# The opening of a two-layer trunk: first modulation on TensorE, early fillers, one-piece scaling

## The chip, the cores and the metric

The kernel runs on one core of one Trainium2 chip. The metric is the device time of one execution, in microseconds; the time of a kernel is the median of its runs.

A core has five engines, each with its own stream of instructions: PE multiplies matrices, DVE and ACT work on tiles element by element (ACT with a table of functions that has to be loaded), POOL is a third such engine, and SP here only issues transfers. Transfers from memory (DMAs) can be issued by SP, ACT and POOL; each issuer has its own queue. Engines meet only where one needs what another has written, or where a buffer has to be given back first.

## The reference

Two layers work on x, 256 tokens by 1024 channels. Each has a token mixer (layer 0 dilated attention, layer 1 gated linear attention) and a gated convolutional feed-forward part. Ahead of each of these four parts x is normalised and modulated by a vector c:

```python
for i in range(DEPTH):                                  # 2 layers
    mod = jax.nn.silu(c) @ w_ada[i] + b_ada[i]          # c: 1024 -> 6 * 1024
    sh1, sc1, g1, sh2, sc2, g2 = split(mod, 6)
    h = rmsnorm(x, norm_mix[i]) * (1.0 + sc1) + sh1
    y = dilated_mixture(h, ...) if i == 0 else gla_mixer(h, ...)   # first step: h @ w_in
    x = x + g1 * y
    h = rmsnorm(x, norm_ffn[i]) * (1.0 + sc2) + sh2
    x = x + g2 * conv_ffn(h, ...)
return rmsnorm(x, norm_final)
```

All data are fp32. What matters here is the start: the mean of squares of x, SiLU of c, the shift and the scale (pieces 0 and 1 of `mod`) of layer 0, and the first columns of h @ w_in, which are the queries, keys and values of the first pair of heads.

## The kernel before

**Layout.** Channels lie on the 128 partitions, tokens along the row. x is one tile `x_all` of 128 x 8 x 256: 8 tiles (kt = 0 to 7) of 128 channels. A weight block for one kt is 128 x 1920 and comes from memory into a buffer of the pool `wraw` (4 buffers, `raw`; the modulation weights `ada_raw` use the same four).

**Products.** A product in fp32 is made of three in the faster format fp32r: each operand is split into a high part and a remainder (`whi`/`wlo` of the weights, `hhi`/`hlo` of h), and high·high, high·low and low·high are summed in PSUM, the memory that PE writes. The weights' high part is a cast on ACT (`split`, L176), the remainder a subtraction on DVE (`low_part`, L188), each in two halves of 960 columns. `mm3` (L203 to L205) is the three products of one block.

**The opening.** c comes as one row of 1024 on one partition (ACT's queue, L86). PE multiplies it by a row of ones, so that all 128 partitions hold all of c (`cb`, L125); ACT applies SiLU (`c_bc`, L126). x comes in two transfers on SP's queue. DVE and ACT square it (L389, L392), DVE adds tiles up (L395), PE sums over partitions with a matrix of 1/1024 (`ms`, L215), and ACT makes `rstd` of it by a logarithm and an exponential (L217, L219); these two need another function table (`exp_ln_after`) than SiLU. Between these, PE makes products that nobody reads (`keep_warm`, L301): three blocks of 4, 3 and 6, and three small products for the rows of the attention's biases (L409), which ACT copies out (L437).

**A step of kt.** SP loads `ada_raw` and `raw`. DVE makes two dot products of 128 x 1024 with `c_bc` (`ada_dot`, L142), one for the scale, one for the shift; ACT makes one column of each (L150, L152). DVE scales x by the column and by `rstd` (`xr`, L287), ACT adds the shift and rounds to the high part `hhi` (L289), DVE makes the remainder `hlo` (L291). PE then makes this tile's products: 6 blocks of 256 columns for queries and keys, three products each (L696), 2 of 384 for the values (L700), and 6 of `mm3`.

**Order.** A scheduler puts the instructions of each engine in the order in which their inputs are due; `with behind(a):` holds an instruction back until `a` has been placed, without a wait on the chip. Transfers of one issuer run in the order written. Banks of PSUM belong to three tags (p: 2, s: 3, t: 3); where `bank` is called without a tag, the next of a fixed cycle is taken.

Of the kernel before, what the change touches and what calls it, by code (L numbers as in the profile page):

```python
# [59 lines left out]
def trunk(ctx: ExitStack, tc: tile.TileContext, I, out):  # L60
# [18 lines left out]

    def exp_ln_after(last):  # L80
# [15 lines left out]
    nc.scalar.dma_start(tab[:32, :], I["rel_bias"])  # L96
    nc.vector.memset(tab[32:33, :], 1.0)
    oh = wspl.tile([P, 2048], F32, tag="whi", name="oh")
    nc.scalar.dma_start(oh[:33, :NROW], I["onehot"])
# [6 lines left out]
    eps = const.tile([P, 1], F32, name="eps")  # L106
    nc.vector.memset(eps, EPS)
    ident = const.tile([P, P], F32, name="ident")
    make_identity(nc, ident)
# [11 lines left out]

    c_bc = const.tile([P, D], F32, name="c_bc")
    for n in range(2):
        ps = bank("cb", "t")
        last_c = mm(ps, ones_d[:1, :], c_row[:1, 512 * n : 512 * n + 512], start=True, stop=True)  # L125
        silu = nc.scalar.activation(c_bc[:, 512 * n : 512 * n + 512], ps, AF.Silu, scale=float(D))  # L126
# [11 lines left out]
    def ada_dot(l, n, s, raw):  # L138
# [5 lines left out]
        )  # L144
        m = state.tile([P, 1], F32, tag=f"mod{l}{piece}{kt}", name="mod")
# [8 lines left out]
        return i, j  # L154
# [119 lines left out]
    @contextmanager  # L274
    def behind(*those):

        with ExitStack() as st:
            for i in those:
                st.enter_context(tc.issue_after(i.ins))
            yield  # L280

# [15 lines left out]
    def keep_warm(n):  # L297

        ps = bank("warm")
        for i in range(n):  # L300
            mm(ps[:, :P], ones_d, ones_d, start=True, stop=True)  # L301

    early_x = [state.tile([P, T + 16], F32, tag=f"ex{k}", name="early_x") for k in range(KT)]
# [78 lines left out]

    sq = wspl.tile([P, 2048], F32, tag="wlo", name="sq").rearrange("p (k t) -> p k t", k=KT)
    with behind(last_c):
        keep_warm(4)
    nc.vector.tensor_tensor(sq[:, 0:4, :], x_all[:, 0:4, :], x_all[:, 0:4, :], op=ALU.mult)  # L389
    with behind(silu):  # L390
        for i in (4, 6):
            last_sq = nc.scalar.activation(sq[:, i : i + 2, :], x_all[:, i : i + 2, :], AF.Square)  # L392
    for n in (0, 4):
        for m in (2, 1):
            last_add = nc.vector.tensor_tensor(sq[:, n : n + m, :], sq[:, n : n + m, :], sq[:, n + m : n + 2 * m, :], op=ALU.add)  # L395
        if n == 0:
            with behind(last_add):
                last_add = scale_terms(0)
    exp_ln_after(last_sq)
    r = rstd_of([sq[:, 0, :], sq[:, 4, :]])  # L400

    rows_ps, at = [], 0
    with behind(norm_ops[0]):
        keep_warm(3)
        for i, (g, n) in enumerate(ROWS):
            c = slice(at, at + n)
            ps = bank("rows", "t")[:16, 0:n]
            rows_ps.append((ps, c))
            last_row = mm(ps, tab[:, 16 * g : 16 * g + 16], oh[:33, c], start=True, stop=True)  # L409
            at += n  # L410
    with behind(last_row):
        keep_warm(6)


    w0, h = [], []
    last = last_add
    for kt in range(KT):
        ada = ada_load(0, kt, 1 if kt else 2)
        with behind(*((last,) if kt else (norm_ops[1], last))):
            dots = [ada_dot(0, kt, 0, ada)]  # L420
        with behind(dots[0][0]):
            dots.append(ada_dot(0, kt, 1, ada))

        def between(scaled, high):

            ahead, term = (dots[1][1], dots[1][1]) if kt == 0 else (dots[0][1], dots[1][1])
            w0.append(split(I["w0"][kt], 15 * P, 1 if kt else 2, after=((ahead,), (high,)), lows=False))
            with behind(scaled):
                return [low_part(w0[-1], 0)]

        h.append(normed(0, 0, r, kt, (dots[1][0],), between))
        with behind(chain[kt][1]):
            last = low_part(w0[kt], 1)
        if kt == 0:
            with behind(copied[0]):
                for ps, c in rows_ps:
                    nc.scalar.copy(rows[:, c], ps)  # L437
        if kt == 1:
            with behind(last):
                last = scale_terms(1)  # L440
    with tc.issue_after(last_load[0].ins):
        nc.sync.dma_start(rows_d, rows)
        nc.sync.dma_start(small[:, C_CW:], I["small"][:, C_CW:])
# [226 lines left out]
    for u in range(NPAIR):  # L670
# [13 lines left out]
        if u == 0:  # L684
            b0 = [bank("pqk", tg) for tg in "ssspp"]
            pqk = [b[:, T * i : T * i + T] for b in b0[:3] for i in range(2)]
            pv = b0[3:]
            b1 = [bank("pqk", "t") for _ in range(3)]
            pqk1 = [b[:, T * i : T * i + T] for b in b1 for i in range(2)]
            for kt in range(KT):  # L690
                s, e = kt == 0, kt == KT - 1

# [803 lines left out]
```

## Time and profile before

| what | value |
|---|---|
| time, median of 3 runs | 747.81 us (747.49 to 748.27) |
| profiled execution | 752.01 us |
| its span, first to last instruction | 750.2 us |
| PE busy | 741.7 us, 99% |
| DVE busy | 648.2 us, 86% |
| ACT busy | 480.6 us, 64% |
| POOL busy | 31.7 us, 4% |
| DMA | 187.20 MB, mean 250 GB/s |
| granted TensorE clock, mean | 0.998 |

The span is of one execution under the profiler, 4.2 us longer than the median of the runs. Busy means that an instruction is under way; a PE that runs at a low clock, or makes products that nobody reads, is as busy as one that works. A row of an engine's order of time gives start, length (both us), engine, line and operation, output <- inputs, sizes, and the number of records put together. In brackets stands how long the engine had waited and for what. "PEld" rows are loads of the stationary operand. The granted clock is a column of the profile that stands apart from the durations.

### The profile page before, as it was taken

To read this page: it belongs to the slowest core of one execution; us is meant where nothing else is said; L and a number is where in the kernel's file an instruction comes from. 1 tells how busy PE (TensorE), PEld (TensorE's weight loads), DVE (VectorE), ACT (ScalarE), POOL (GpSimd) and SP (SyncE) were. 2 spreads that over 40 slices of the span, in tenths; PEclk is the share of its full clock that TensorE was granted. 3 is DMA by queue.
4 is the path that set the end of the run, shared out by engine and by line. 5 is a ranking of instruction groups with operands and counts; after the bars stand their busy time and mean duration, and the time that the engine had idled before them with its cause. 6 is when DMAs were issued, how large, how long until landed. Compare 5 with 4: busy or idle time off the path is not lost.

```text
span 750.2 us, 15928 instructions
## 1 busy us (share of the span) xinstructions
PE 741.7 (99%) x6344; PEld 726.6 (97%) x6344; DVE 648.2 (86%) x1195; ACT 480.6 (64%) x943; POOL 31.7 (4%) x57
## 2 busy tenths in 40 slices
PE   8999999999999999999999999999999999999997
PEld 5999999999999999999999999999999999999996
DVE  6997998989988859999998886898969999997592
ACT  5556775555656658776766565865768766666551
POOL 0002001101101010000000000000010000000100
PEclk9999999999999999999999999999999999999999
DMA  9998789888788438877746997776757766874621
GB/s 349 399 304 294 241 317 369 270 315 280 263 309 284 132 117 295 311 281 240 256 128 207 315 341 243 256 266 224 261 194 274 281 223 236 211 179 157 205 100 57
DMA packets 39481, 187.20 MB, mean 250 GB/s; under 512 B 9020, under 2 KB 11708, under 8 KB 25838
## 3 DMA queue, kind: packets, MB, share of 16 engines
q1 hardware_dynamic: 39024, 185.73, 71.4%
q8 instruction: 50, 0.82, 0.4%
q10 hardware_dynamic: 382, 0.45, 0.2%
q14 instruction: 25, 0.20, 0.1%
HBM read 185.06 MB, written 1.10 MB: 248 GB/s over the span
## 4 chain that ended last, share of the span: by engine, by line
PE 98%; DVE 1%; ACT 0%; DMA 0%; issue 0%; DVEq 0%; ACTq 0%
PE pab L204 10%; PE pab L205 10%; PE pab L203 10%; PE pqk L203 6%; PE pqk L205 6%; PE pqk L204 6%; PE pd L204 5%; PE pd L205 5%; PE pd L203 5%; PE pv L203 4%; PE pv L205 4%; PE pv L204 4%; PE pqk L696 2%; PE py L203 2%; PE py L205 2%; PE py L204 2%
## 5 line engine op out<-in xcount | busy, mean ns | idle before, releaser
L176 ACT CAST whi<-raw 128x1024 fp32r<-128x1024 f32 (+4 forms) x264 | 237.8, 945 | 107.0 <-PE pab L204 55.0
L182 DVE TENSOR_TENSOR wlo<-raw,whi 128x1024 fp32r<-128x1024 f32 (+5 forms) x248 | 263.8, 1092 | 30.6 <-ACT whi L176 29.8
L205 PE MATMUL pab<-hhi,wlo 128*128 128x256 f32 x672 | 185.0, 276 | 0.0
L204 PE MATMUL pab<-hlo,whi 128*128 128x256 f32 x672 | 184.9, 277 | 0.0
L203 PE MATMUL pab<-hhi,whi 128*128 128x256 f32 x672 | 183.1, 277 | 0.0
L204 PEld LDWEIGHTS pab<-hlo,whi 128*128 128x128 f32 x672 | 126.1, 188 | 0.2
L205 PEld LDWEIGHTS pab<-hhi,wlo 128*128 128x128 f32 x672 | 126.2, 188 | 0.0
L203 PEld LDWEIGHTS pab<-hhi,whi 128*128 128x128 f32 x672 | 125.1, 188 | 0.1
L142 DVE CUSTOM_DVE_ANT_0 ada_raw<-ada_raw,c_bc 128x1024 f32<-128x1024 f32 x96 | 114.3, 1230 | 4.6 <-DMA ada_raw<-in_w_ada 4.4
L203 PE MATMUL pqk<-hhi,whi 128*128 128x256 f32 x374 | 102.4, 279 | 0.0
L204 PE MATMUL pqk<-hlo,whi 128*128 128x256 f32 x374 | 101.8, 277 | 0.0
L205 PE MATMUL pqk<-hhi,wlo 128*128 128x256 f32 x374 | 101.3, 278 | 0.0
L205 PE MATMUL pd<-ghi,wlo 128*128 128x256 f32 x308 | 84.9, 276 | 0.0
L204 PE MATMUL pd<-glo,whi 128*128 128x256 f32 x308 | 84.9, 276 | 0.0
L203 PE MATMUL pd<-ghi,whi 128*128 128x256 f32 x308 | 84.7, 276 | 0.0
L203 PEld LDWEIGHTS pqk<-hhi,whi 128*128 128x128 f32 x374 | 69.9, 188 | 0.2
L204 PEld LDWEIGHTS pqk<-hlo,whi 128*128 128x128 f32 x374 | 69.9, 188 | 0.0
L205 PEld LDWEIGHTS pqk<-hhi,wlo 128*128 128x128 f32 x374 | 69.2, 188 | 0.1
L204 PEld LDWEIGHTS pd<-glo,whi 128*128 128x128 f32 x308 | 57.8, 188 | 0.0
L205 PEld LDWEIGHTS pd<-ghi,wlo 128*128 128x128 f32 x308 | 57.8, 188 | 0.0
L203 PEld LDWEIGHTS pd<-ghi,whi 128*128 128x128 f32 x308 | 57.7, 188 | 0.0
L204 PE MATMUL pv<-wlo,hhi 128*128 128x384 f32 (+2 forms) x160 | 52.8, 332 | 0.0
(272 smaller groups left out, 1440.8 us busy)
## 6 DMA issues: line engine op xcount, KB each, us to landing
raw<-in_w_up SPq DMA_DIRECT2D x42, 1024.0 KB, 4.9
ada_raw<-in_w_ada SPq DMA_DIRECT2D x29, 1024.0 KB, 6.0
raw<-in_w_down SPq DMA_DIRECT2D x28, 704.0 KB, 5.1
ada_raw<-in_w_ada SPq DMA_DIRECT2D x38, 512.0 KB, 6.8
raw<-in_wqk SPq DMA_DIRECT2D x18, 1024.0 KB, 6.7
raw<-in_wv SPq DMA_DIRECT2D x14, 768.0 KB, 7.0
raw<-in_w SPq DMA_DIRECT2D x7, 960.0 KB, 6.1
raw<-in_w_v_b SPq DMA_DIRECT2D x6, 768.0 KB, 5.0
```

Of the source, the lines that this page charges most:

```text
L142: i = dotted[0] = nc.vector.tensor_tensor_reduce(w, w, c_bc, op0=ALU.mult, op1=ALU.add, scale=1.0, scalar=0.0, accum_out=dot,)
L176: copied[0] = nc.scalar.copy(part(hi[:, c]), part(raw[:, c]))
L182: last_lo[0] = nc.vector.tensor_tensor(part(lo[:, c]), part(raw[:, c]), part(hi[:, c].bitcast(F32)), op=ALU.subtract)
L203: mm(ps, a[0], b[0], start=start, stop=False)
L204: mm(ps, a[0], b[1], start=False, stop=False)
L205: return mm(ps, a[1], b[0], start=False, stop=stop)
L696: mm(pqk[i], w[a], h[kt][b], start=s and i % 2 == 0 and (a, b) == (0, 0), stop=e and i % 2 == 1 and b == 1)
```

## The change

**c by a diagonal tile.** c comes as a column tile of 128 x 8 (`c_col`, still on ACT's queue, L95): channel 128 k + p in row p, column k. ACT applies SiLU to these 8 columns and writes them into the first column of each of 8 groups of 32 columns that POOL has set to zero (`c_sel`, L98). Then the EXP/LN table is loaded. DVE multiplies the identity matrix by each column (`spread`, L148, two instructions of 512 columns), PE multiplies that by the matrix of 1/1024 (`cb`, L155), and ACT copies it out times 1024 (`c_bc`, L439), behind its squares.

**First two tiles' modulation on PE.** For tiles 0 and 1 `ada_first` holds the weights of scale and shift with the inputs on partitions, 8 blocks of 256 columns. `first_products` (L198) multiplies each by `c_sel`'s 32 columns; the four blocks of a half go to four groups of 32 columns of PE's array, so that they write four groups of 32 output rows. `first_parts` (L204) copies the 128 x 256 sums out, `first_sums` (L210) adds over partitions by a product with a column of ones, and ACT makes the two columns as before (L182, L184). The bytes and places in SP's queue are those of the `ada_raw` they replace; the second tile's, too, is now loaded in two halves. Tiles 2 to 7 keep DVE's dots.

**Fillers.** One block of eleven stands ahead of everything on PE (L138); the three blocks of 4, 3 and 6 are gone.

**x scaled in one piece.** DVE scales tiles 1 to 7 by `rstd` in one instruction into `all_early` (L541), which was eight tiles and is now one. Per tile, ACT makes `hhi` (L555) and the unrounded `hf` (L558) with the modulation's scale and shift as the instruction's factor and bias; DVE subtracts (`hlo`, L562). Tile 0 is made by DVE alone (L530 to L532).

**Smaller.** The tables `tab` and `oh` are loaded from POOL's queue instead of ACT's. The squares are pieces of 512 columns, and the mean is four products of 256 instead of two. Tile 0's weights are cast in 384, 576 and 960 columns. The first products' loops move ahead (`front`, `front_values`, `back`), with the second tile's modulation between the first tile's.

```diff
-    c_row = wspl.tile([P, 2048], F32, tag="whi", name="c_row")
-    nc.scalar.dma_start(c_row[:1, :D], I["c"])
+    oh = wspl.tile([P, 2048], F32, tag="whi", name="oh")
+    c_col, c_sel = oh[:, D : D + KT], oh[:, D + T : D + 2 * T].rearrange("p (k j) -> p k j", k=KT)
+    nc.scalar.dma_start(c_col, I["c_col"])
+    nc.gpsimd.memset(c_sel, 0.0)
...
-    nc.scalar.dma_start(tab[:32, :], I["rel_bias"])
+    nc.gpsimd.dma_start(tab[:32, :], I["rel_bias"])
...
-    nc.scalar.dma_start(oh[:33, :NROW], I["onehot"])
+    nc.gpsimd.dma_start(oh[:33, :NROW], I["onehot"])
...
+    last_warm = keep_warm(11)
+    silu = nc.scalar.activation(c_sel[:, :, 0], c_col, AF.Silu)
+    exp_ln_after(silu)
     for n in range(2):
-        ps = bank("cb", "t")
-        last_c = mm(ps, ones_d[:1, :], c_row[:1, 512 * n : 512 * n + 512], start=True, stop=True)
-        silu = nc.scalar.activation(c_bc[:, 512 * n : 512 * n + 512], ps, AF.Silu, scale=float(D))
+        c = slice(512 * n, 512 * n + 512)
+        nc.vector.tensor_tensor(spread[:, c].rearrange("p (k j) -> p k j", j=P),
+                                ident.unsqueeze(1).to_broadcast([P, 4, P]),
+                                c_sel[:, 4 * n : 4 * n + 4, 0:1].to_broadcast([P, 4, P]), op=ALU.mult)
+    with behind(last_warm):
+        for n in range(2):
+            c_ps.append(bank("cb", "s"))
+            last_c = mm(c_ps[n], ones_d, spread[:, 512 * n : 512 * n + 512], start=True, stop=True)
...
+    def first_products(raw, ps, ks, *after):
+        for k in ks:
+            j = slice(32 * (k % 4), 32 * (k % 4) + 32)
+            with behind(*after):
+                last = mm(ps[j, 0:T], c_sel[:, k, :], raw[:, T * k : T * k + T], start=(k < 4), stop=(k >= 4))
+        return last
+    def first_parts(ps, *after):
+        part = tmp.tile([P, T], F32, tag="sqacc", name="part")
+        with behind(*after):
+            i = nc.vector.tensor_copy(part, ps[:, 0:T])
+        return part, i
+    def first_sums(kt, ps, part, *after):
+        for i in range(2):
+            with behind(*after):
+                last = mm(ps[:, T + i : T + i + 1], part[:, P * i : P * i + P], one, start=True, stop=True)
+        return last, [modulation(0, piece, kt, ps[:, T + i : T + i + 1]) for i, piece in enumerate((1, 0))]
...
-    early_x = [state.tile([P, T + 16], F32, tag=f"ex{k}", name="early_x") for k in range(KT)]
+    all_early = state.tile([P, KT, T + 16], F32, name="early_x")
+    early_x = [all_early[:, k, :] for k in range(KT)]
...
-    with behind(last_c):
-        keep_warm(4)
...
-    with behind(norm_ops[0]):
-        keep_warm(3)
...
-    with behind(last_row):
-        keep_warm(6)
...
+            with behind(last):
+                last = nc.vector.tensor_tensor(all_early[:, 1:, 0:T], x_all[:, 1:, :],
+                                               r.unsqueeze(1).to_broadcast([P, KT - 1, T]), op=ALU.mult)
...
+        high = nc.scalar.activation(hi, early_x[kt][:, 0:T], AF.Identity, scale=a[:, 0:1], bias=sh[:, 0:1])
+        hf = tmp.tile([P, T], F32, tag="xr", name="xr")
+        with behind(high):
+            nc.scalar.activation(hf, early_x[kt][:, 0:T], AF.Identity, scale=a[:, 0:1], bias=sh[:, 0:1])
+        with behind(dots[1][0] if kt >= FIRST else last):
+            last = low_part(w0[kt], 0)
+        with behind(last):
+            last = nc.vector.tensor_tensor(lo, hf, hi[:, :].bitcast(F32), op=ALU.subtract)
```

How the order of instructions moves is shown at three places. The first is PE's start, up to the first tile's products with the high parts. A row gives line, operation, output <- inputs, size and number; `warm` are the fillers, `cb` is c, `ms` the mean of squares, `rows` the bias rows, `dots` the first modulation, `pqk` the products that count. Before:

```order
L125 MATMUL cb<-c_row,ones_d 128x512 x2
L301 MATMUL warm<-ones_d 128x128 x4
L215 MATMUL ms<-sq,ones_d 128x256 x2
L301 MATMUL warm<-ones_d 128x128 x3
L409 MATMUL rows<-oh,tab 16x512
L409 MATMUL rows<-oh,tab 16x128 x2
L301 MATMUL warm<-ones_d 128x128 x6
L696 MATMUL pqk<-hhi,whi 128x256 x6
```

The same stretch of PE after the change (`oh` beside `ada_raw` is `c_sel`, which lies in the tile of that name):

```order
L138 MATMUL warm<-ones_d 128x128 x11
L155 MATMUL cb<-spread,ones_d 128x512 x2
L447 MATMUL ms<-sq,ones_d 128x256 x2
L198 MATMUL dots<-ada_raw,oh 32x256 x4
L447 MATMUL ms<-sq,ones_d 128x256 x2
L198 MATMUL dots<-ada_raw,oh 32x256 x4
L210 MATMUL dots<-eps,part 128x1 x2
L463 MATMUL rows<-oh,tab 16x512
L463 MATMUL rows<-oh,tab 16x128 x2
L480 MATMUL pqk<-hhi,whi 128x256 x6
```

All fillers now stand first, c's products need `spread`, and the first `pqk` product follows the bias rows at once.

The second place is ACT in a step of kt from 2 on, from one step's first instruction to the next one's. Before:

```order
L150 ACTIVATE mod<-dot,one_b,small 128x1
L176 CAST whi<-raw 128x960
L152 ACTIVATE mod<-dot,small 128x1
L289 ACTIVATE hhi<-xr,mod 128x256
L176 CAST whi<-raw 128x960
```

After:

```order
L233 CAST whi<-raw 128x960
L182 ACTIVATE mod<-dot,one_b,small 128x1
L233 CAST whi<-raw 128x960
L184 ACTIVATE mod<-dot,small 128x1
L555 ACTIVATE hhi<-early_x,mod 128x256
L558 ACTIVATE xr<-early_x,mod 128x256
```

Both casts of the weights now stand ahead of the high part of h, and the unrounded h (`xr`) is ACT's too.

The third place is POOL's start, after the change:

```order
masks.py:197 MEMSET ident 128x128
L98 MEMSET oh 128x256
L108 DMA tab<-in_rel_bias 32x48
L110 DMA oh<-in_onehot 33x768
masks.py:199 ISA
masks.py:199 AFFINE_SELECT ident<-ident 128x128
```

The zeros of `c_sel` (the row that writes `oh`) and the two transfers stand between the two halves of the identity; before, three small memsets stood there.

More of the change, by code (lines that the diff above doesn't have):

```diff
@@ L383, in load_bias @@
         return both
+    FIRST = 2
     sq = wspl.tile([P, 2048], F32, tag="wlo", name="sq").rearrange("p (k t) -> p k t", k=KT)
-    with behind(last_c):
-        keep_warm(4)
[L389 to L398, printed above, removed]
@@ L399, in trunk @@
[L399 to L412 removed]
+    firsts = [first_load(0)]
@@ new lines, in trunk @@
+    with behind(last_add):
+        last_terms = scale_terms(0)
+    mean, dots = bank("ms", "p"), bank("dots", "s")
+    for at, ks in ((0, range(4)), (4, range(4, KT))):
+        with behind(last_c):
+            for i in (at, at + 1):
+                last_c = mm(mean[:, :T], ones_d, sq[:, i, :], start=(i == 0), stop=(i == 5))
+        last_c = first_products(firsts[0], dots, ks, last_c)
+    ln = tmp.tile([P, T], F32, tag="ln", name="ln", bufs=2)
+    with behind(last_copy):
+        nc.scalar.activation(ln, mean[:, :T], AF.Ln, bias=eps[:, 0:1])
@@ new lines, in trunk @@
+    r = tmp.tile([P, T], F32, tag="rstd", name="rstd", bufs=2)
+    last_r = nc.scalar.activation(r, ln, AF.Exp, scale=-0.5)
+    part, last_part = first_parts(dots, last_terms)
+    last_dots, last_mods = first_sums(0, dots, part)
+    rows_ps, at = [], 0
+    for i, (g, n) in enumerate(ROWS):
+        c = slice(at, at + n)
+        ps = bank("rows", "t")[:16, 0:n]
+        rows_ps.append((ps, c))
+        with behind(last_dots):
+            last_row = mm(ps, tab[:, 16 * g : 16 * g + 16], oh[:33, c], start=True, stop=True)
+        at += n
@@ new lines, in trunk, with front @@
+    b0 = [bank("pqk", tg) for tg in "ssspp"]
+    pqk = [b[:, T * i : T * i + T] for b in b0[:3] for i in range(2)]
+    pv = b0[3:]
+    second_ps = bank("dots", "t")
+    b1 = [bank("pqk", "t") for _ in range(3)]
+    pqk1 = [b[:, T * i : T * i + T] for b in b1 for i in range(2)]
+    BOTH = ((0, 0), (1, 0), (0, 1))
+    def front(kt, terms, tiles=range(2 * NG), *after):
+        s, e = kt == 0, kt == KT - 1
+        for a, b in terms:
+            for i in tiles:
+                w = w0_parts(kt, P * i)
+                with behind(*after):
+                    last = mm(pqk[i], w[a], h[kt][b], start=s and i % 2 == 0 and (a, b) == (0, 0), stop=e and i % 2 == 1 and (a, b) == terms[-1])
+        return last
@@ new lines, in front_values, with back @@
+    def front_values(kt, terms, *after):
+        s, e = kt == 0, kt == KT - 1
+        wv = w0_parts(kt, 6 * P, NG * P)
+        for a, b in terms:
+            for t in range(2):
+                with behind(*after):
+                    last = mm(pv[t][:, : NG * P], h[kt][a][:, P * t : P * t + P], wv[b], start=s and (a, b) == (0, 0), stop=e and (a, b) == BOTH[-1])
+        return last
+    def back(kt, tiles, *after):
+        for i in tiles:
+            with behind(*after):
+                last = mm3(pqk1[i], w0_parts(kt, 9 * P + P * i), h[kt], kt == 0 and i % 2 == 0, kt == KT - 1 and i % 2 == 1)
+        return last
```

142 lines of the change are left out of this document (94 added, 48 removed).

## The prediction

> **What bounds the kernel now.** I read the page first, for which engine the time belongs to, then the order of time on PE over the first 24 us, then DVE and ACT there, and last the DMA landings.
>
> ```profile
> span 750.2 us, 15928 instructions
> PE 741.7 (99%) x6344; PEld 726.6 (97%) x6344; DVE 648.2 (86%) x1195; ACT 480.6 (64%) x943; POOL 31.7 (4%) x57
> ```
>
> PE is busy for all but 8.5 us. So a gain can come only from PE work that is not the kernel's product: fillers, waits under a busy mark, and work at a low clock. All that stands at the start. PE's rows (start, length, both us; one instruction of fp32 leaves two records, one of fp32r one):
>
> ```profile
> 8.50 2.33 PE L215 MATMUL ms<-sq,ones_d 128*128 128x256 f32 x4
> ...
> 12.05 2.74 PE L409 MATMUL rows<-oh,tab 33*16 33x512 f32 x6
> ...
> 14.72 2.93 PE L301 MATMUL warm<-ones_d 128*128 128x128 f32 x12
> ...
> 17.30 1.63 PE L696 MATMUL pqk<-hhi,whi 128*128 128x256 f32 x6
> ...
> 18.72 1.29 PE L696 MATMUL pqk<-hhi,wlo 128*128 128x256 f32 x6
> ...
> 23.73 0.87 PE L696 MATMUL pqk<-hhi,whi 128*128 128x256 f32 x6
> ...
> 55.44 0.87 PE L696 MATMUL pqk<-hhi,whi 128*128 128x256 f32 x6
> ```
>
> The first product that counts starts at 17.30. Its six take 1.63 us, the six at 23.73 only 0.87: about 0.21 us from start to start against 0.12. The clock column reads 1.00 for all of it, but the durations say that PE ran at half rate until some time in the row at 18.72. From 23.73 on the steps follow each other without a gap: (55.44 - 23.73) / 6 = 5.28 us each, which is PE's own work. The time of the kernel is thus fixed by when step 1 starts, as long as nothing makes PE wait later. Why PE starts at 17.30 is seen on DVE and ACT:
>
> ```profile
> 9.47 1.22 DVE L142 CUSTOM_DVE_ANT_0 ada_raw<-ada_raw,c_bc 128x1024 f32<-128x1024 f32 x1
> ...
> 10.62 1.22 DVE L142 CUSTOM_DVE_ANT_0 ada_raw<-ada_raw,c_bc 128x1024 f32<-128x1024 f32 x1
> ...
> 12.11 0.48 DVE L287 SCALAR_TENSOR_TENSOR xr<-x_all,mod,rstd 128x256 f32<-128x256 f32 x1 [0.26 <-ACT mod L150]
> ```
>
> ```profile
> 11.70 0.37 ACT L150 ACTIVATE mod<-dot,one_b,small 128x1 f32<-128x1 f32 x1
> 11.98 0.28 ACT L152 ACTIVATE mod<-dot,small 128x1 f32<-128x1 f32 x1
> ...
> 13.05 0.50 ACT L289 ACTIVATE hhi<-xr,mod 128x256 fp32r<-128x256 f32 x1
> ```
>
> The first hhi is written at 13.55, but the bias rows and two blocks of fillers hold PE until 17.3, half of it at half rate.
>
> **The change, part by part.** *Prices at full clock.* Four 256-column records of fp32 start 0.22 us apart; where two column groups share the array, records start in pairs, 0.21 us a pair; a PSUM copy of 256 columns is 0.42.
>
> ```profile
> 278.53 1.03 PE L215 MATMUL ms<-sq,ones_d 128*128 128x256 f32 x4
> ```
> ```profile
> 101.90 1.08 PE L591 MATMUL po<-pt,v 128*64 128x256 f32 x8
> ```
> ```profile
> 58.78 0.42 DVE L615 COPY k<-pqk 128x256 f32<-128x256 f32 x1 [3.16 <-ACT q L615]
> ```
>
> Eight records in 1.08 are four pairs. Four groups in the array are not in this form in the trace: between full overlap (0.43 us for four instructions) and none (1.7), I take overlap, as the two groups overlap whole; both ends stay in the range.
>
> *c.* It now lands as 128 short pieces, passes SiLU on 8 columns, and the diagonal tile is built by DVE. Rows for it:
>
> ```profile
> 0.74 2.09 DMA c_row<-in_c
> ```
> ```profile
> small<-in_small ACTq DMA_DIRECT2D x1, 71.0 KB, 5.4
> ```
> ```profile
> 2.65 1.28 ACT L126 ACT_TABLE_LOAD   x1 [2.65 <-issue]
> ...
> 525.91 1.28 ACT L1321 ACT_TABLE_LOAD   x1
> 527.20 0.60 ACT L1321 ACTIVATE r<-pr 128x512 f32<-128x512 f32 x1
> ```
>
> c's one row landed at 2.83; `small`, 128 pieces like the new column, 5.4 us after its issue. I take 3.1, since c is the queue's first and x's pieces are not ahead of it; the other end is 0.74 + 5.4 = 6.1. The table load now waits for c: 3.1 + 1.28 + 0.3 for SiLU = 4.7. The next load follows at once; a function ran 0.01 us after a load at 527.20, so I add nothing. The Trainium skill ("ScalarE: Activation LUTs", What ACT_TABLE_LOAD costs) gives about 1.38 us of drain with each switch; the trace has no such gap, and with it the two loads would put the squares 2.8 us later and take most of the gain. POOL now issues two DMAs ahead of finishing ident. No DMA of POOL is in the trace; SP's and ACT's issues are the nearest (0.33 to 0.87 us, the row of 0.33 is below), so from nothing to 1.8 us for both, ident at 1.4 to 3.2: hidden behind SiLU at 4.7. Spread is two tensor-tensors of 512 columns, 0.6 each (half of the dot's 1.22 for 1024) -> 5.9; two squares and an add, 0.6 each -> 7.7.
>
> *PE until the first sums.* Eleven fillers at half rate from 1.2 us, 22 records of 0.21 (2.93 over 12 with its tail, above) -> 6.0. If the clock then rises, as it did some 4.6 us after dense fillers began at 14.72, c's two 512-column products take 4 x 0.43 = 1.7 -> 7.75, and two of the mean 0.85 -> 8.6. First modulation products need the halves of the first tile:
>
> ```profile
> DMA to landing us min/median/max: 7.0/7.4/7.7
> ```
>
> Issued at 1.65 and about 2.1 (the first two modulation loads), they land at 8.65 and 9.8; bytes and order are kept. So 0.43 -> 9.1, mean 0.85 -> 9.95, second half 0.43 and a tail of 0.2 -> 10.6. Copy 0.42 -> 11.05, two column sums with fp32 weights 0.6 -> 11.7, modulation (hf can start 0.41 after it, as 12.11 did after 11.70) -> 12.2, hf 0.48 and hi 0.4 -> 13.1. The bias rows (2.74 at half rate, 1.3 at full) fill that gap. **First product at 13.3 instead of 17.3, at full clock.**
>
> *Step 0 on PE.* 5.28 of products; 0.86 for the second tile's eight modulation products; 0.65 for its sums; and a wait: DVE does lo (0.48), two wlo (1.08 each, start to start), the one-piece scaling of 1792 columns (2.0 by the dot's rate) and a copy, until 18.45, where PE arrives at 18.1. 13.3 + 5.28 + 0.86 + 0.65 + 0.35, and 0.15 for changes of the array's division = 20.6. Step 1 started at 23.73: **-3.1 us**.
>
> *Steps 2 to 7.* The scaled x costs DVE nothing per tile now, hi and hf are two ACT instructions behind the second modulation. A step before:
>
> ```profile
> 21.16 1.22 DVE L142 CUSTOM_DVE_ANT_0 ada_raw<-ada_raw,c_bc 128x1024 f32<-128x1024 f32 x1
> ...
> 25.46 1.16 DVE L188 TENSOR_TENSOR wlo<-raw,whi 128x960 fp32r<-128x960 f32 x1
> 26.54 1.22 DVE L142 CUSTOM_DVE_ANT_0 ada_raw<-ada_raw,c_bc 128x1024 f32<-128x1024 f32 x1
> ```
> ```profile
> 22.72 0.98 ACT L176 CAST whi<-raw 128x960 fp32r<-128x960 f32 x1
> 23.61 0.29 ACT L152 ACTIVATE mod<-dot,small 128x1 f32<-128x1 f32 x1
> ```
>
> DVE's step was 5.38 us. Now, from the first dot's start t: second modulation at t + 2.45 (23.61 - 21.16), hi ready at t + 3.3, hf t + 3.75, lo to t + 4.15, second wlo, next dot at t + 5.2. That is under PE's 5.28. But DVE starts step 2 at 22.45 (18.45, wlo, then lo after hf at 20.9, wlo), not 21.16: the lead of 4.5 us that DVE had over PE is gone. hi of tile 2 is ready at 25.8, PE comes at 25.9. A buffer is given back by wlo or the dot, so loads are issued about 1 us later too:
>
> ```profile
> 37.39 0.33 SPq L169 DMA_DIRECT2D raw<-in_w  x1
> ...
> 42.76 0.33 SPq L169 DMA_DIRECT2D raw<-in_w  x1
> ```
> ```profile
> 44.71 0.99 ACT L176 CAST whi<-raw 128x960 fp32r<-128x960 f32 x1 [0.41 <-DMA raw<-in_w]
> ```
>
> The weights of step 6 landed 7.2 us after 37.39 and ACT was already waiting for them. From such a landing to hi of its step it is the cast's 0.9, the modulation, the second cast, 0.29 and 0.5: 3.0 us. With the same landing, hi of step 6 comes at 47.6, where PE would be at 47.0: 0.6 late, and nearly the same at step 7. With loads a microsecond later and 7.2 us each it is 1.4; with 5.3, as other steps have by their rows, nothing. I take 0.8 between nothing and 1.4: **+0.8**.
>
> *The rest.* Fewer dots (four of 1.22) and no xr on DVE leave it 5 us freer, off PE's path. Small DMAs move from ACT's queue to POOL's; their data are needed at 11.7, far behind. The order behind the opening is the same; PSUM banks of later tiles turn by four places, for which I take 0, within 0.3 either way.
>
> Sum: -3.1 + 0.8 = -2.3 us. The profiled execution took 752.0 (span 750.2), 4.2 over the median of the runs, 747.8; I carry the difference over: **745.5**. What a measurement here tells from no change is 0.2%, 1.5 us.
>
> **Rivals.** *A, the clock falls back.* Between 9 and 13 us PE works in pieces with waits between. In the trace PE ran from 6.6 to 12 with gaps and was still at half rate at 17.3, so broken work does not raise it; nothing shows how it is lost. If it is half rate at 13.3 and takes another 3.5 to 5 us, PE loses half of that, 1.7 to 2.5, and the time is 747.6: no change. The Trainium skill ("TensorE: Matmul & The Clock Gate", Part 1) says one idle window of about 3.4 us takes the rate back; the trace has no such case ahead of its end, and my longest expected wait is under 1 us.
> *B, c comes late (the other side).* Its 128 pieces queue like `small`'s and land at 6.1, 3.0 us later than I took. SiLU, spread, squares and mean are one chain without slack, so all moves: step 1 at 23.6, DVE's step 2 at 25.4, loads of steps 6 and 7 another 3 us later, and PE waits at step 7 for 0.7 to 2: 748.9. It decides against the change from about 5.5 on; against it speaks that c is first on its queue.
> *C, no late loads.* Landings at 5.3 us: the whole 3.1 stays, 744.7. It is the upper half of my forecast.
> *D, four groups do not overlap.* 1.3 us more for each tile's eight products beyond what is covered, 2.5 in all: 748.0, no change. The pairs at 101.90 speak against it.
>
> **Chances.** Forecast with C: 0.60, its own range 744.0 to 746.2 (C's 744.7 with the banks' 0.3 and 0.4 for a step 0 without its wait; late loads at their full 1.4). A 0.13, D 0.07, and a late c of one to two us 0.08, nearly all of it within 0.2%. B or anything like it 0.12, of which 0.10 is beyond +1.5. So faster 0.61, same 0.29, slower 0.10. The range, 744.0 to 748.6, leaves out B's worse half and a gain of over 3.8, which needs what no row shows.
>
> **What would show it.** Right: the first pqk product near 13.3 with six in under 0.9 us; dots records in groups of four; step 1 at 20 to 21 and no wait of PE over 1 us until 58. Wrong: SiLU behind 5.5; pqk records 0.21 apart behind 13; PE waiting for hhi or whi at steps 6 and 7 for more than 1.5 us together; DVE's steps above 5.4.

## The result, and the profile after

The changed kernel takes 755.2 us (median of its runs, 753.1 to 759.0), the kernel before 748.0: a ratio of 1.010, interval 1.0076 to 1.0124. One run of 4244 us here, and one of 1901 us among the twelve of the experiment without fillers below, are left out as disturbed. The forecast was 745.5, with 748.6 as its upper end. The profiled execution took 758.3 us, with a span of 756.5.

```profile
span 756.5 us, 16017 instructions
...
PE 742.9 (98%) x6384; PEld 727.2 (96%) x6384; DVE 643.6 (85%) x1186; ACT 484.7 (64%) x951; POOL 35.1 (5%) x60
```

PE is now idle for 13.6 us instead of 8.5. PE's order of time through the opening, then the steps that waited:

```profile
1.20 4.23 PE L138 MATMUL warm<-ones_d 128*128 128x128 f32 x22 [1.20 <-DVE eps L121]
7.51 3.54 PE L155 MATMUL cb<-spread,ones_d 128*128 128x512 f32 x4 [2.09 <-DVE spread L148]
10.84 1.21 PE L447 MATMUL ms<-sq,ones_d 128*128 128x256 f32 x4
...
14.80 0.61 PE L210 MATMUL dots<-eps,part 128*128 128x1 f32 x4 [0.55 <-DVE part L204]
15.34 1.47 PE L463 MATMUL rows<-oh,tab 33*16 33x512 f32 x6
16.92 0.94 PE L480 MATMUL pqk<-hhi,whi 128*128 128x256 f32 x6
...
19.98 1.48 PE L480 MATMUL pqk<-hhi,wlo 128*128 128x256 f32 x6
...
25.52 0.87 PE L480 MATMUL pqk<-hhi,whi 128*128 128x256 f32 x6
...
48.02 0.96 PE L480 MATMUL pqk<-hhi,whi 128*128 128x256 f32 x6 [1.20 <-ACT hhi L555]
...
60.58 0.98 PE L480 MATMUL pqk<-hhi,whi 128*128 128x256 f32 x6 [1.43 <-ACT hhi L555]
```

The first product that counts starts at 16.92, not at 13.3; the six at 19.98 take 1.48 us, which is half rate; step 1 starts at 25.52, not at 20.6; PE waits at steps 5 and 7. That much is a chain that starts late, as ACT shows:

```profile
5.15 1.28 ACT L143 ACT_TABLE_LOAD   x1 [5.15 <-DMA oh<-in_c_col]
6.44 0.21 ACT L143 ACTIVATE oh<-oh 128x8 f32<-128x8 f32 x1
```

c's 128 pieces landed at 5.1, and the table load stood behind them. PE sat idle for 2.09 us, and c's products then took 3.54 us, nearly all of it at half rate. But the two profiles, 752.0 and 758.3, are both of executions that lie 3 to 4 us above the medians of their kernels. The comparison has to be made between usual executions, and it then looks different.

### The profile page after: what moved, and what is told of

It reads as the page before. It is cut to its first block, busy times and chain, and to the rows that moved or that the text cites. A ratio compares the mean times of both kernels' runs of the same rounds, so it can differ in the third digit from the quotient of the medians.

```text
span 756.5 us, 16017 instructions
## 1 busy us (share of the span) xinstructions
PE 742.9 (98%) x6384; PEld 727.2 (96%) x6384; DVE 643.6 (85%) x1186; ACT 484.7 (64%) x951; POOL 35.1 (5%) x60
## 4 chain that ended last, share of the span: by engine, by line
PE 89%; DMA 5%; DVE 3%; ACT 2%; issue 0%; DVEq 0%; ACTq 0%; SPq 0%
PE pab L261 10%; PE pab L260 10%; PE pab L262 10%; PE pqk L260 6%; PE pqk L262 5%; PE pqk L261 5%; PE pd L261 4%; PE pd L260 4%; PE pd L262 4%; PE pv L261 4%; PE pv L262 4%; PE pv L260 4%; DMA raw<-in_w 2%; PE py L260 2%; PE py L261 2%; PE py L262 2%
## 5 line engine op out<-in xcount | busy, mean ns | idle before, releaser
L233 ACT CAST whi<-raw 128x1024 fp32r<-128x1024 f32 (+5 forms) x262 | 236.0, 945 | 119.6 <-PE pab L261 54.6
L171 DVE CUSTOM_DVE_ANT_0 ada_raw<-ada_raw,c_bc 128x1024 f32<-128x1024 f32 x92 | 109.4, 1229 | 4.8 <-DMA ada_raw<-in_w_ada 4.8
L260 PE MATMUL pqk<-hhi,whi 128*128 128x256 f32 x374 | 104.6, 280 | 0.0
L262 PE MATMUL pqk<-hhi,wlo 128*128 128x256 f32 x374 | 103.9, 278 | 0.0
L261 PE MATMUL pqk<-hlo,whi 128*128 128x256 f32 x374 | 103.8, 277 | 0.0
```

Of the source, the lines that this page charges most:

```text
L171: i = dotted[0] = nc.vector.tensor_tensor_reduce(w, w, c_bc, op0=ALU.mult, op1=ALU.add, scale=1.0, scalar=0.0, accum_out=dot,)
L233: copied[0] = nc.scalar.copy(part(hi[:, c]), part(raw[:, c]))
L260: mm(ps, a[0], b[0], start=start, stop=False)
L261: mm(ps, a[0], b[1], start=False, stop=False)
L262: return mm(ps, a[1], b[0], start=False, stop=stop)
```

## The experiments

**The kernel before, profiled again.** No edit, two executions.

> The kernel before, unchanged, profiled a second time, since its profiled execution (752.0) lay 4.2 us above its median. Theory 'the clock's turn is a matter of luck, and the profiled execution was an unlucky one': in an execution of 747.8 PE comes to full rate a window earlier than 19.6, the first product that counts starts at 13.6 to 14.5 instead of 17.3, step 1 at 19.5 to 20.5 instead of 23.7, and the rest is alike. The gain that was forecast from 17.3 to 13.3 is then one that most executions of the kernel before have already. Rival: the first product starts at 17.3 again and the 4 us lie in waits behind it or at the end.

> The same kernel before once more, for a third execution. Both theories expect what they expect of the second; two turns of the clock out of three would show how far the turn moves from one execution to the next.

The first took 747.50 us, near the median, the second 750.27. PE's order of time in the first:

```profile
9.90 0.83 PE L301 MATMUL warm<-ones_d 128*128 128x128 f32 x6
10.66 1.47 PE L409 MATMUL rows<-oh,tab 33*16 33x512 f32 x6
12.05 1.60 PE L301 MATMUL warm<-ones_d 128*128 128x128 f32 x12
13.42 0.94 PE L696 MATMUL pqk<-hhi,whi 128*128 128x256 f32 x6
...
18.75 0.87 PE L696 MATMUL pqk<-hhi,whi 128*128 128x256 f32 x6
```

The rise of the clock came at 9.9 (six fillers in 0.83 us; it was 2.93 for twelve at half rate). The bias rows took 1.47 instead of 2.74, the last fillers 1.60 instead of 2.93, and the first useful product starts at 13.42 instead of 17.30, step 1 at 18.75 instead of 23.73. In the second the clock rose at 19.0 and the first product stood at 16.59. So the profiled execution on which the prediction rests was a rare one (of the 73 timed runs of the kernel before, 10 took over 750 us and none 752.0), and what the change was to win from 17.3 to 13.3 is there already in a usual execution of the kernel before. An early start is also not kept whole: with step 1 at 18.75 PE waits for 0.9 us in steps 1 to 7, with step 1 at 23.73 for nothing, so that 5.0 us at step 1 are 4.05 at the values behind step 7 (56.65 for 60.70).

**The changed kernel, profiled again.** No edit; once alone, once with five rounds beside a variant below.

> The changed kernel unchanged, for a second profile near its median (755.2), since the first one (758.3) lay above it. Expected by the theory of several costs: c lands at 5 again, c's products at half rate, first pqk product at 15.5 to 17, step 1 at 23.5 to 25.5, waits of 1.5 to 3 us at steps 5 to 7; the difference to the first profile is a window of half rate less, or the wait of 1.5 us at the end.

> The changed kernel unchanged, on the same chip beside the one with 14 fillers, for a comparison of like with like: 754.5 to 755.5, with the fetch at 3 to 4.3 us after the issue and the wait of 1.5 us in its profile.

754.76 us, and 755.84 (ratio 1.0094, 1.0074 to 1.0113). The second one's profiled execution, 755.68:

```profile
7.58 1.99 PE L155 MATMUL cb<-spread,ones_d 128*128 128x512 f32 x4 [1.32 <-DVE spread L148]
...
13.99 0.60 PE L210 MATMUL dots<-eps,part 128*128 128x1 f32 x4 [0.55 <-DVE part L204]
14.53 1.47 PE L463 MATMUL rows<-oh,tab 33*16 33x512 f32 x6
16.11 1.05 PE L480 MATMUL pqk<-hhi,whi 128*128 128x256 f32 x6
16.96 1.48 PE L480 MATMUL pqk<-hlo,whi 128*128 128x256 f32 x6
...
24.69 0.87 PE L480 MATMUL pqk<-hhi,whi 128*128 128x256 f32 x6
```

Here, and in the execution of 754.76, c's products ran at full rate (1.99 us): their half rate belongs to the execution of 758.3 alone.

Set against the execution of 747.50, event by event (us):

| event | before | changed | lost so far |
|---|---|---|---|
| first useful product | 13.42 | 16.11 | 2.7 |
| step 1 | 18.75 | 24.69 | 5.9 |
| values of the next pair, behind step 7 | 56.65 | 62.96 | 6.3 |
| last mean of squares | 728.19 | 736.24 | 8.05 |

Four places, then: 2.7 ahead of the first product, 3.25 within step 0, 0.4 in steps 1 to 7, 1.7 behind that. The next experiments take them one by one.

Step 0 takes 8.6 us in all three profiles of the changed kernel, and in all three it has a stretch of 3.4 us at half rate (18.0 to 21.4, 16.0 to 19.5, 16.8 to 20.2). Whether an execution has such a stretch can be told from its mean granted clock: in the 20 profiles of this case the mean is 0.998 or more where the clock stays up once it has risen, 0.996 or 0.997 with one stretch of 3.4 us, and 0.993 to 0.995 with two. (Before the first rise the column reads 1.00, although PE runs at half rate; behind it, it agrees with the durations.) By this measure the clock was lost in every one of the changed kernel's fourteen executions (0.993 to 0.997), and in none of the kernel before.

**SiLU's table early.**

```diff
+    nc.scalar.preload_act_table_set("silu_and_others")
```

> The changed kernel with one line more: ACT loads the SiLU table right behind its two DMA issues, instead of behind c's landing (the load stood at 5.15, c landed at 5.05). Theory 'late c sets the opening': SiLU moves from 6.44 to about 5.2, spread, c's products and the mean 1.25 us earlier, and PE's idle stretch shrinks from 2.09 to 0.85 us, so that the clock may stay up and c's products take 1.7 instead of 3.4 us; first pqk product at 13.6 to 15.5 instead of 16.92, step 1 at 22 to 24 instead of 25.5. Loads of steps 3 to 7 come earlier by as much, and the waits of PE at steps 5 and 7 (2.6 us together) keep their size or shrink: 750 to 753 instead of 755.2. Rival 'the place of tile 1's modulation alone matters': the step starts earlier, the buffers of tile 1 still come back late, PE waits longer at steps 5 and 7, 754 to 755.

752.71 us (ratio 1.0066, 1.0040 to 1.0092). SiLU ran at 5.25, as soon as c was there, and the first product stood at 14.85, 1.26 us ahead of the changed kernel's usual 16.11, as expected of late c. The median is 2.5 us better; the rest of that fits a clock that stayed up more often (mean 0.998 or 0.999 in four of the six executions). Its profiled execution (757.1, not a usual one) lost time elsewhere: PE waited 2.28 us ahead of step 7, and after that wait the clock was down from 59.1 to 62.5.

**More fillers.** `keep_warm(11)` becomes `keep_warm(21)`.

> The changed kernel with 21 fillers instead of 11, so that PE has work until the spread tile is there at 7.5. Theory 'the idle 2.09 us took the clock back': c's two products take 1.7 us instead of 3.54, the mean waits for DVE's squares instead (10.5), first pqk product 1 to 1.5 us earlier, 753.5 to 754.5 instead of 755.2. Rival 'the clock falls for another reason': c's products still take 3.4 us, or the clock falls again around 18, and the time is unchanged within 0.5.

754.06 us (1.0077, 1.0056 to 1.0099). In the profiled execution c's products took 1.98 us and step 0 ran at full rate:

```profile
7.61 1.98 PE L155 MATMUL cb<-spread,ones_d 128*128 128x512 f32 x4
...
16.14 0.93 PE L480 MATMUL pqk<-hhi,whi 128*128 128x256 f32 x6
...
23.13 0.87 PE L480 MATMUL pqk<-hhi,whi 128*128 128x256 f32 x6
```

Step 0 is 7.0 us here and 8.6 in the changed kernel's three profiles, so that the stretch at half rate costs 1.55 us. The first product comes no earlier than in a usual execution with eleven fillers (16.11), and c's products were at full rate there too; so this run does not show that the idle stretch ahead of them matters in most executions. The clock stayed up in three of its six (0.998 or 0.999).

**Second tile's modulation early.**

```diff
             done = front(0, ((0, 0), (0, 1)), range(2 * NG), last_row)
+            done = first_products(firsts[1], second_ps, range(KT), done)
...
             done = front_values(0, ((0, 0), (1, 0)), done)
+            done, _ = first_sums(1, second_ps, part, done)
```

> The changed kernel with the second tile's eight modulation products moved ahead: behind the first twelve products of step 0 (about 18.5 instead of 21.8), its column sums behind the first value products, DVE's copy of them ahead of the one-piece scaling. Nothing else moves. Theory 'tile 1's place holds buffers back': the buffer of its modulation weights comes free at about 19.5 instead of 22.5, the buffer of its weights at about 25 instead of 27.3; the loads that follow are issued 2 to 3 us earlier; PE's waits at steps 5 and 7 (1.2 and 1.4 us) vanish: 752 to 753 instead of 755.2, first pqk product unchanged at 16.9. Rival 'everything is late because c is late': loads move, but the waits stay over 1.5 us together, time within 1 us of 755.2.

755.72 us (1.0099, 1.0076 to 1.0122): no gain. The buffer of the modulation weights came back 1.8 us earlier (next load at 20.3 instead of 22.1), but DVE's step 2 began at 26.25 against 26.40. The scheduler had put the second tile's casts behind its modulation, so that ACT stood idle ahead of them:

```profile
21.52 0.35 ACT L182 ACTIVATE mod<-dots,one_b,small 128x1 f32<-128x1 f32 x1 [3.75 <-PE dots L210]
...
21.92 1.89 ACT L233 CAST whi<-raw 128x960 fp32r<-128x960 f32 x2
```

So this run says little of the theory: the early buffer was had, the early high part was not. In a version below (the last of those with c in 8 rows) the casts stood ahead, and DVE's step 2 came 0.9 us earlier (21.73 for 22.62).

**Both.**

> Both of the above: SiLU's table loaded early and tile 1's modulation products early. If the two costs are separate, the gains add: step 1 at 22 to 24 and no wait of PE over 0.5 us until step 7, 747 to 750, about the kernel before. If one cause is behind both, it is no better than the better of the two alone.

753.52 us (1.0071, 1.0050 to 1.0092), no better than the table alone. Here the casts did stand ahead of the second tile's modulation, and in its profile steps 1 to 6 follow each other without a wait of PE, up to one of 1.58 us ahead of step 7. But the clock stayed up in only one of the six executions, against four with the table alone; at 1.55 us each that alone may hide a gain of under 1 us.

**c in 8 rows.** c is loaded as 8 rows of 512 bytes and turned by one product with the identity; the table is loaded early.

```diff
+    c8 = const.tile([KT, P], F32, name="c8")
+    nc.scalar.dma_start(c8, I["c8"])
...
+    keep_warm(5)
+    ct = bank("ct", "t")
+    last_ct = mm(ct[:, :KT], c8, ident[:KT, :KT], start=True, stop=True)
+    with behind(last_ct):
+        last_warm = keep_warm(4)
+    silu = nc.scalar.activation(c_sel[:, :, 0], ct[:, :KT], AF.Silu)
```

> The changed kernel with c loaded as 8 rows of 512 bytes, turned into the column tile by one small product with the identity among the fillers (five ahead, four behind), and SiLU's table loaded early. Theory 'the 128 short pieces of c are what is late': the 8 rows land at 2.9 like the one row of before (2.8), SiLU runs at 3.6 to 4.2 instead of 6.44, spread at 4 to 5.3, modulation at 11.2 to 12.2 instead of 15.45 (the second half of the weights lands at 8.85), first pqk product at 12.5 to 13.5, step 1 at 20 to 21.5; waits at steps 5 and 7 under 1 us; 748 to 750. Rival 'the order behind tile 0 is what costs': the start is as early as that, but PE still waits for 2 us or more at steps 5 to 7, since the buffers come back later than before all the same: 750 to 752.

> The version with c in 8 rows unchanged, for a second profile, since its profiled execution (751.25) lay 2.2 us under its median. Theory 'clock': in an execution of 753 or more a window of half rate of 3.4 or 6.8 us lies between 14 and 40 us and step 1 starts at 22 or later. Rival 'transfers': the clock holds as in the first profile, step 1 starts at 21, and the time goes in waits for weights at steps 5 to 7 or at the end (1.5 us).

> The same once more, for a third profile; both theories as for the second.

753.49 us (1.0083, 1.0063 to 1.0102). Three profiles (751.25, 752.94, 752.77) have the same opening within 0.02 us; the first:

```profile
13.90 0.94 PE L486 MATMUL pqk<-hhi,whi 128*128 128x256 f32 x6
...
20.92 0.87 PE L486 MATMUL pqk<-hhi,whi 128*128 128x256 f32 x6
```

The column's late landing, with the table load behind it, was worth 2.2 us of the first product (1.26 by the table alone). With c early and the clock up, the opening comes out as the prediction had it: 13.9 for 13.3, 20.9 for 20.6. And still it is 2.2 us behind step 1 of the kernel before (18.75). The values of the next pair come 1.9, 4.1 and 2.7 us late: with all loads 2 us later, PE waits for weights in some executions and not in others. In these three the rival, transfers, was right, and the clock stayed up. In the timed runs both happen: the two longest of the six, 756.97 and 754.63 us, have a mean clock of 0.995 and 0.997, the others 0.998 or more.

**Fillers in its gaps.** Two fillers ahead of the column sums, one behind the bias rows.

> The version with c in 8 rows, with two fillers between the second modulation products and their column sums and one behind the bias rows, where PE waited (0.55 and 0.3 us). Theory 'the new opening is too thin on PE to hold the clock': products with few rows or columns (bias rows, column sums) do not count as work, so in many executions a window of about 3.4 us is judged idle and step 0 or 1 runs at half rate; with the gaps filled, fewer executions lose it: median 751 to 752.5 instead of 753.5 and a smaller spread. Rival 'the late part of the executions comes from transfers': no change, 753 to 754 with executions up to 757.

753.94 us (1.0071). The clock stayed up in all five executions (0.999 or 1.000), and the longest is 754.55 instead of 756.97; so the spread shrank as the theory had it. The median did not fall: the profiled execution waits 1.09, 1.55 and 1.71 us for the high part at steps 3, 5 and 7.

**ACT's order of before.** In the version with c in 8 rows the second cast of a step stands behind the high part again.

```diff
-            w0.append(split(I["w0"][kt], 15 * P, after=((), ()) if kt < FIRST else ((dots[0][1],), ()), lows=False))
+            w0.append(split(I["w0"][kt], 15 * P, after=((), ()) if kt < FIRST else ((dots[0][1],), high), lows=False))
```

> The version with c in 8 rows, with ACT's order of the kernel before in steps 2 to 7: modulation, first cast, modulation, high part, second cast (and the unrounded h behind that). Theory 'with both casts ahead of the high part a late weight costs PE more': from the landing of a step's weights to its high part it is 1.8 to 2.2 us instead of 3.0, PE's waits between steps 3 and 7 (up to 3.2 us in the four profiles) shrink to under 1 us, 751.5 to 752.5 instead of 753. Rival 'loads come late because DVE gives buffers back late': the remainder of h now waits for the second cast, DVE's step grows above 5.4 us, and the time is the same or longer, 753 to 755.

> All repairs of the changed opening at once: c in 8 rows, SiLU's table early, second tile's modulation products early, ACT's order of before. If late c, late buffers and ACT's order are each a cost of their own, it comes to 749.5 to 751.5, within 3 us of the kernel before; what then is left is PE's own extra work in step 0 (1.7 us) and DVE's late start of step 2. If one of them is the whole, it is no better than 753.

759.58 us (1.0144, 1.0122 to 1.0165); with the second tile's modulation early as well, 757.16 (1.0122). Both worse, and DVE shows why (the first of the two):

```profile
29.52 0.43 DVE L575 TENSOR_TENSOR hlo<-xr,hhi 128x256 fp32r<-128x256 f32 x1 [1.06 <-ACT xr L571]
...
31.02 1.22 DVE L177 CUSTOM_DVE_ANT_0 ada_raw<-ada_raw,c_bc 128x1024 f32<-128x1024 f32 x1
...
37.22 1.22 DVE L177 CUSTOM_DVE_ANT_0 ada_raw<-ada_raw,c_bc 128x1024 f32<-128x1024 f32 x1
```

The remainder of h waits 1.06 us for the unrounded h behind the second cast; DVE's step is 6.20 us instead of 5.30, PE's follows (6.19). The changed kernel's order, both casts first, is the right one for a remainder that needs two results of ACT. These two and the next also have one wait of 1.95 us of PE at 94 to 99, for a copy of the next pair's keys that the scheduler has put further back on DVE; it was not followed up. The first one's profile (761.64 us) lost the clock twice as well, in step 0 (14.5 to 17.9) and behind that wait.

**The scaling alone, in the kernel before.** One piece on DVE, high part and unrounded h on ACT, everything else as before.

> The kernel before with one part of the change alone: x scaled in one piece on DVE behind the first tile's weights, high part and unrounded h on ACT for tiles 1 to 7; dots, fillers and c as before. The piece is 2.0 us on DVE ahead of the second tile's dots, so its high part comes at 19.5 to 20.5 and step 1 starts 1 to 1.8 us later than 18.75; DVE's step falls from 5.38 to about 4.9, so nothing is lost behind that and up to 0.9 us of waits goes away: 748.0 to 749.5 against 747.9. Rival 'it is free': 747.5 to 748.0.

756.18 us (1.0112, 1.0098 to 1.0125), a miss: 8.35 us, not 1. PE waited 1.72 us ahead of step 1, as expected for a piece of 2.0 us in front of the second tile's dots. But DVE's step grew instead of shrinking, from 5.38 to 5.85:

```profile
31.44 1.16 DVE L188 TENSOR_TENSOR wlo<-raw,whi 128x960 fp32r<-128x960 f32 x1 [0.20 <-ACT whi L176]
32.76 0.43 DVE L445 TENSOR_TENSOR hlo<-xr,hhi 128x256 fp32r<-128x256 f32 x1 [0.16 <-ACT xr L440]
33.65 1.16 DVE L188 TENSOR_TENSOR wlo<-raw,whi 128x960 fp32r<-128x960 f32 x1 [0.46 <-ACT whi L176]
34.73 1.22 DVE L142 CUSTOM_DVE_ANT_0 ada_raw<-ada_raw,c_bc 128x1024 f32<-128x1024 f32 x1
```

DVE has 0.48 us less to do per step and waits 0.82 for ACT. Before, its own scaling filled the time in which ACT cast. The values of the next pair come 4.7 us late, and most of the rest of the 8.35 is in four waits behind them (3.3 us), of which the wait of 1.95 for the moved copy comes from the new order and not from the scaling itself.

**Without fillers; with more of them, in the kernel before.** The three blocks taken out; or four fillers more, ahead of c's products.

> The kernel before with its three blocks of fillers taken out and nothing in their place. Theory 'the fillers hold the clock up at the first useful product': PE reaches 13.4 cold in most executions, step 0 runs at half rate for 2 to 3.4 us and costs 1 to 1.7 us more, 749 to 750 with little spread. Rival 'they only cost': bias rows end earlier and the time is unchanged, 747.5 to 748.2.

> The kernel before with one block of four fillers more, ahead of c's products on PE (from 1.2 to 2.9 us, where PE was idle until 2.96). If the clock's turn needs a stretch of dense work, it comes at 4.5 to 8 in every execution, and the times lose their upper ones (750 to 752): 747.0 to 747.8 with a range under 1 us. Rival 'the turn depends on work just ahead of it alone': no change, 747.8 with executions of 750 and more among them.

Without: 749.52 us (1.0016, 1.0002 to 1.0031). PE was cold when it came to the first product, and step 0 took 8.1 us instead of 5.3:

```profile
13.73 1.65 PE L691 MATMUL pqk<-hhi,whi 128*128 128x256 f32 x6
...
21.82 0.87 PE L691 MATMUL pqk<-hhi,whi 128*128 128x256 f32 x6
```

With four more: 748.77 (1.0016, 1.0005 to 1.0027). They put c's products 0.9 us later (3.19 for 2.27), and the first useful product came 1.3 us later (14.71). The early rise that was expected (4.5 to 8) did not come: the clock rose at 11.5, and executions of up to 751.8 us stayed. Early fillers are no gain where c is early, and the blocks that the change took out were worth 1.2 to 1.7 us.

**The end: 14 fillers instead of 11.** In the changed kernel.

> The changed kernel with 14 fillers instead of 11. The three more lie in the time in which PE waits for the spread tile (1.5 to 2.1 us), so nothing else is moved; but PE's program is 12 instructions longer, and the fetch of 16 KB of it that fell 3.1 to 4.0 us after the issue of the last weights comes earlier (0.6 in the version with c in 8 rows and three fillers more). Theory 'that fetch holds up one of the sixteen parts of the last weights': the wait of about 1.5 us ahead of the last mean of squares is under 0.6, and the time is 0.8 to 1.5 us under that of the unchanged one beside it. Rival 'the wait has another cause': it stays at 1.5, times within 0.5.

753.95 us (1.0071, 1.0050 to 1.0092), 1.9 under the unchanged one beside it. First the unchanged one's last mean of squares, and then the same row with 14 fillers:

```profile
736.24 0.38 PE L1040 MATMUL ms<-ones_d,sqacc 128*128 128x2 f32 x2 [1.56 <-DVE sqacc L287]
```
```profile
733.33 0.38 PE L1040 MATMUL ms<-ones_d,sqacc 128*128 128x2 f32 x2 [0.15 <-DVE sqacc L287]
```

DVE was late there because it had waited for the last weights, 2.50 us against 1.10:

```profile
715.62 2.44 DVE L1009 TENSOR_TENSOR raw<-raw,gate_row 128x256 f32<-128x256 f32 x7 [2.50 <-DMA raw<-in_w_last]
```
```profile
712.75 2.44 DVE L1009 TENSOR_TENSOR raw<-raw,gate_row 128x256 f32<-128x256 f32 x7 [1.10 <-DMA raw<-in_w_last]
```

The DMA queues in the 4 us in which these weights landed, without and then with three fillers more:

```profile
q1 hardware_dynamic: 162, 1.05, 76.0%
q8 instruction: 1, 0.02, 1.5%
```
```profile
q1 hardware_dynamic: 161, 1.04, 78.0%
```

A fetch of 16 KB of instructions lies in that stretch in the one and not in the other, where it came 0.6 us after the issue. In the one the sixteenth part of the weights was reported 6.12 us after the issue, the fifteenth at 4.65; in the other the last at 4.72. So three fillers that take no time gave 1.4 us back at the other end of the kernel. In this profile the clock also stayed up through step 0 (7.0 us), as it did in three of its six executions (0.998 or 0.999) and in none of the six beside it, so that not all of the 1.9 is the fetch. Over all profiles: the late sixteenth part (1.1 to 1.8 us) stands in nine of the eleven with the fetch 3.1 to 4.3 us after the issue, and in none of the others; so the two can meet there, and need not.

## Why the prediction was wrong

*The sum's base.* The step that failed first is the one that carried the profiled execution's 4.2 us over to the median as if they were spread evenly. They lay in the very stretch of the change: 17.30 and 23.73 were of an execution in which the clock rose late. Against the usual 18.75, the predicted step 1 at 20.6 is 1.9 us later, not 3.1 earlier. The range was built on the same base. The prediction also has half of PE's time up to 17.3 at half rate; the rows that it shows are at half rate throughout, and the clock rose at 19.6.

*c.* Taken at 3.1 because c is first on its queue; it landed at 5.1, nearer to the other end (6.1). SiLU was done at 6.65 to 6.7 instead of 4.7. That is rival B, in place and side. What it was worth is shown, together with the table load that waited for it: 2.2 us of the first product, which with DVE's and PE's pieces on top stood at 16.1 instead of 13.3.

*The clock.* Rival A, at 0.13, happened in all three profiles of the changed kernel and, by their mean clock, in all its fourteen executions; in step 0 it cost 1.55 us. The reason against it was that the clock is lost only to an idle stretch, and that PE was to wait for under 1 us at a time. It left out that PE may issue without pause and the time yet not count. In the profile after, PE's clock rises at 4.4, falls at 7.8, rises at 11.2, falls at 18.0 and rises at 21.4: turns 3.41 or 6.83 us apart. The idle 2.09 us fit the first fall, which the other two profiles, idle for 1.48 and 1.32 us, do not have. But from 14.6 to 18.0 PE was idle for only 0.3 us; 2.0 us of the rest went to column sums of one column and to bias rows on 33 rows and 16 columns, and the clock fell.

That these two kinds of product do not count was argued and not tried by itself, but the traces bear it out against the rival that idle time alone does it. Cut into pieces of 3.41 us from the first rise to the last 8 us, the 20 profiles have ten pieces that end in a fall. PE was busy in them for 1.1 to 3.1 us, with other products for at most 1.5. Pieces that kept the clock had as little as 1.8 us of busy time, and never under 1.4 of other products. So the outcome turns on which products fall into one piece. In the version with c in 8 rows, 1.44 us kept the clock in one profile and, in the run with ACT's order of before, 0.75 lost it with the same opening.

The prediction had a sign of this before its eyes. It reads PE's work from 6.6 to 12 as broken by gaps, to explain why the clock did not rise; PE was idle there for 0.05 us. The Trainium skill ("TensorE: Matmul & The Clock Gate", Part 1) has the window at 3413 ns and free-running, so that the turn falls differently from one execution to the next; these traces agree, with turns at multiples of 3.41 us and rises at 9.9, 19.0 and 19.6 in three executions of the kernel before. That spread is over two windows wide, so a free phase alone does not give it: in the two late ones the windows in which the bias rows lay (9.4 to 16.2 in the execution of 752.0) went by without a rise.

*Step 0.* 5.28 + 0.86 + 0.65 + 0.5 = 7.3 was the sum; 7.02 measured where the clock stays up. This is the lasting price of PE's modulation: 1.7 us against 5.33 before. The four column groups overlapped as taken.

*Steps 2 to 7.* DVE's step was 5.30 to 5.38 (predicted 5.2), and the loss 0.4 us in the usual execution above, -0.3 to 4.3 over all profiles that keep the changed kernel's order on ACT (predicted 0.8, within 0 and 1.4). The mechanism was right, a late DVE makes late loads; its size varies more.

*The table loads.* 0.01 to 0.02 us from a load's end to the function, as taken; POOL's identity at 2.9, within 1.4 and 3.2.

*The end.* 1.4 us from an instruction fetch that the longer PE program moves: not in the prediction at all.

By its own terms the sum becomes: 747.5; + 1.9 (20.6 against the usual 18.75); + 2.8 (first product at 16.1 for 13.3); + 1.55 (half rate); - 0.3 (step 0); + 0.4 (steps 1 to 7); + 1.7 (the rest, 1.4 of it the fetch) = 755.6, against 755.7 of the execution that is set out above. What is left of the loss in the version with c in 8 rows is 5.5 us by the medians. Its three profiles are 3.75 to 5.4 us over the execution of 747.50: 1.9 to 4.1 up to the values of the next pair (2.2 of it there at step 1), 1.1 to 1.5 in waits behind them, and 1.55 at the end in one of the three. Why the waits for weights differ by 2 us between executions of one program stays open, and the modulation on PE was not run alone, without the other parts of the change.

## What to carry to other kernels

Before a gain is read off a profile, set its time against the median of the runs: where it lies above, find what is unusual in it, or take a second one, since that may be the very thing the change is to remove. Fillers that seem to keep an engine from its work may be what keeps its clock; take them out alone, and see. And moving work from one engine to another is judged by the chain it lengthens: the modulation by PE needed a copy, column sums and a column of c, and came at 12.4 at best, where DVE's dots had it at 10.9. Compare the mean clock of the runs, too, before a difference of medians is put down to one cause.

## What was not expected of the hardware

Products on few rows or columns kept PE busy and let the clock fall (14.6 to 18.0, above). In the kernel before, bias rows seem to have held its rise back in the same way: from 9.4 to 12.8 PE was busy for 3.36 us, 0.77 of it with them, and the clock stayed down. Twelve instructions more on PE at 5 us moved a 16 KB fetch at 710 us from 4.1 to 0.6 us behind a transfer's issue, and the transfer's end by 1.4 us; fetches of this size come some 15 us apart all through the kernel. The Trainium skill ("Runtime: NRT & Kernel Launch", Instruction fetch mechanics) says that instructions come in blocks of 16 KiB by a DMA queue of their own; the profile's queue agrees (50 packets, 0.82 MB), and what the runs add is that a block can hold up a transfer of data.
